# The up projection of a transformer block by seven block products in place of eight

## The chip, the cores and the metric

One core of a Trainium2 chip. The metric is the device time of one execution in microseconds, the median of several runs. One further execution was profiled; its rows carry line numbers of the kernel.

## The reference

One layer of a streaming encoder, on 512 tokens of width 2048, in float32:

```
h = rms_norm(x, pre_mix_g);  z = h @ w_in                       # q, k, v of 8 heads, and the pooled part
m = concat(chunked_attention(z), multiscale_pool(z)) @ w_o
x = x + rms_norm(m, post_mix_g)
h = rms_norm(x, pre_ffn_g)
up = causal_dwconv(h @ w_up, conv_w, conv_b)                    # w_up 2048 x 11264, 3 taps along tokens
y = (gelu(up[..., :5632]) * up[..., 5632:]) @ w_down            # w_down 5632 x 2048
x = x + rms_norm(y, post_ffn_g)
```

## The kernel before

Every matrix product runs on TensorE in the type float32r, each operand split in a high part (rounded by ScalarE, `split`, L127) and a low part (the rest, by VectorE, L128). `mm3` (L143 to L145) multiplies high by high, high by low and low by high, three matmuls into the same bank of PSUM. Each matmul loads 128 x 128 weights and streams up to 512 columns.

Activations lie transposed: 16 tiles of 128 channels by 512 tokens, high and low (`hT`, here called gT). The up projection makes 22 units. A unit is 256 columns of the gate half of w_up and the 256 columns that they are multiplied with; a half unit is one of these two. For a half unit `up` takes four weight tiles of 4 x 128 rows by 256 columns (512 KB each) from a list whose loads run four tiles ahead (`Weights`: SP issues the load into `raw4`, 5 buffers; the split goes to `w4`, 8 buffers, so 4 pairs), and makes 16 x 2 x 3 = 96 matmuls of 512 tokens into two banks. `conv` (L696 to L700) then multiplies by the norm's factor R on VectorE, and adds the three taps on ScalarE and VectorE; `gate` adds the gelu, `product` multiplies the two parts and has POOL store the unit to DRAM (`gd`). Unit 0 is made earlier, beside the norm.

`residual` runs eight times after units 4 to 11: it loads half a token block of x and of the mixing's output, adds them on VectorE and stores them, three blocks to `out` and the last one to `x2d`.

The product with w_down already works by seven products of blocks for eight (Strassen's scheme in Winograd's form), 20 units in five groups: `right` loads blocks of w_down (1 MB, `raw1`, `raw2`), sums them on VectorE and splits them (`wh`, `wl`); `left` does the same with the stored units; `multiply` makes 24 matmuls of 512 columns; `keep_product` has POOL add the products to sums in DRAM by adding DMAs. The first two products (`firsts`) are made right behind the up projection, before the memory of the up stage is given to the pool `p4`. The last two units are multiplied plainly at the end (`last`), block by block, with the last norm; three token blocks reach `out` by adding stores from POOL, the fourth is added to x2 on VectorE.

The order of TensorE's instructions is the order of the program. That of the other engines is chosen by the framework's scheduler when the kernel is built, from priorities in program order and from what is ready; each engine then runs its own list strictly in that order. Buffers are handed out by tag, so that a load waits until the users of an older tile of its tag are done.

Of the kernel before, what the change touches and what calls it, by code (L numbers as in the profile page):

```python
# [15 lines left out]
P = 128  # L16
# [12 lines left out]
WARM = 9  # L29
CU = 4  # L30
# [43 lines left out]
def encoder_layer(ctx: ExitStack, tc: tile.TileContext, x, xT, vecs, rel, post_ffn,  # L74
# [129 lines left out]
    NU = KF // 2  # L204
# [7 lines left out]
    R = const.tile([P, S], F32, name="R")  # L212
# [267 lines left out]
    x2d = dram.tile([P, D], F32, name="x2d")  # L480

    with tc.tile_pool(name="p2", bufs=2, reuse_waits="tile") as p2:
# [102 lines left out]
        for kb in range(KD):  # L585
            if kb % 4 == 0:
                w = [weights.get(f"w{p}0_{kb // 4}") for p in range(2)]
            if kb + 2 < KD:
                x2(kb + 2)
            for p in range(2):  # L590
                for j in range(2):
                    mm3(ups[p][j], part(w[p], kb % 4, slice(j * P, (j + 1) * P)), blk(hT, kb),
                        kb == 0, kb == KD - 1)
# [26 lines left out]
    later = {}  # L620

    def weight(tag, bufs, n, name):

        if n % (bufs + 1) == bufs:
            return later[tag](name, F32R)
        return pr.tile([P, CU, S], F32R, tag=tag, bufs=bufs, name=name)

    def right(c, cc):

        def load(j, l):  # L630
            b = later["raw2"](f"b{j}{l}") if j else raw1(f"b{j}{l}")
            r, cs = 256 * CU * c, slice(l * C + cc * S, l * C + (cc + 1) * S)
            nc.sync.dma_start(b, w_down[r:r + 256 * CU, cs].rearrange(
                "(u j p) n -> p u j n", j=2, p=P)[:, :, j, :])
            return b

        b = {}
        order = yield
        while True:
            i = order  # L640
            for jl in {1: (11, 12), 7: (22,), 6: (22,), 3: (22,), 2: (21,), 4: (21,)}.get(i, ()):
                if jl not in b:
                    b[jl] = load(jl // 10 - 1, jl % 10 - 1)
            if c == cc == 0 and i == 2:
                b[22] = load(1, 1)
            if i == 5:
                nc.vector.tensor_sub(b[11], b[11], b[12])  # L647
            if i == 7:
                nc.vector.tensor_sub(b[12], b[22], b[12])  # L649
            if i == 6:  # L650
# [4 lines left out]
            n = weight.n = getattr(weight, "n", -1) + 1  # L655
            hi, lo = weight("wh", 3, n, "bh"), weight("wl", 2, n, "bl")
            split(hi, lo, v)
            order = yield hi, lo
# [33 lines left out]
    with tc.tile_pool(name="p3", bufs=2, reuse_waits="tile") as p3:  # L692
        def conv(ps, b, tag):
            v = [col(V_CONV, 4 * b + i) for i in range(4)]
            z = p3.tile([P, S], F32, tag="z", name="z")
            nc.vector.tensor_mul(z, ps, R)  # L696
            c = p3.tile([P, S], F32, tag=tag, name=tag)
            nc.scalar.activation(c, z, AF.Identity, scale=v[2], bias=v[3])
            nc.vector.scalar_tensor_tensor(c[:, 1:], z[:, :S - 1], v[1], c[:, 1:], op0=ALU.mult, op1=ALU.add)
            nc.vector.scalar_tensor_tensor(c[:, 2:], z[:, :S - 2], v[0], c[:, 2:], op0=ALU.mult, op1=ALU.add)  # L700
            return c

        def up(u, p, between=None):
            ps = [bank(f"up{u}_{p}_{j}") for j in range(2)]
            for i in range(4):
                w = weights.get(f"w{p}{u}_{i}")
                for kb in range(4 * i, 4 * i + 4):
                    for j in range(2):
                        mm3(ps[j], part(w, kb % 4, slice(j * P, (j + 1) * P)), blk(hT, kb), kb == 0, kb == KD - 1)
                if between and i == 0:  # L710
                    between()
            return ps

        def gate(u, ps):
            a = []
            for j in range(2):
                a.append(conv(ps[j], 2 * u + j, "ca"))
                nc.scalar.activation(a[j], a[j], AF.Gelu_apprx_tanh)
            return a

        def product(u, a, ps):
            g = p3.tile([P, 2, S], F32, tag="g", name="g")
            for j in range(2):
                nc.vector.tensor_mul(g[:, j, :], a[j], conv(ps[j], KF + 2 * u + j, "cb"))
# [5 lines left out]

        def spread2():
            spread(psr, rt)
            nc.vector.tensor_copy(R, psr)

        def residual(t, i):
# [5 lines left out]
            nc.sync.dma_start(x2d[:, cs] if t == NT - 1 else out[t * P:(t + 1) * P, cs], xr)  # L741
# [17 lines left out]

        g1 = up(1, 0, spread2)  # L760
        product(0, gate(0, ups[0]), ups[1])
        product(1, gate(1, g1), up(1, 1))
# [5 lines left out]
        a = gate(NU - 1, up(NU - 1, 0))  # L768
        last = up(NU - 1, 1)

        rights = right(0, 0)
        next(rights)
        firsts = [(i, l, rights.send(i)) for i, l in zip(ORDER0, first_left())]
        product(NU - 1, a, last)
# [3 lines left out]
    with tc.tile_pool(name="p4", bufs=2, reuse_waits="tile") as p4:  # L778
# [8 lines left out]
        later["wh"], later["wl"] = ring("wh", (CU, S), 1), ring("wl", (CU, S), 1)  # L787
# [3 lines left out]
        for r in (slot_h, half_g, later["wl"], later["wh"], raw2, scratch, slot_l, product_part):  # L791
# [81 lines left out]
        spare = [lambda: raw1("wb", F32R)] + [lambda: later["wh"]("wb", F32R), lambda: later["wl"]("wb", F32R)]  # L873
        for k, (cb, i) in enumerate((cb, i) for cb in range(1, 4) for i in range(2)):
            if k < 3:
                w = spare[k]()
            else:
                w = pr.tile([P, CU, S], F32R, tag=("wh", "wl", "wh")[k - 3], bufs=(3, 2, 3)[k - 3], name="wb")
            ws[i, cb] = last_w(i, cb, w)
# [33 lines left out]
        def last(t, cols):  # L913
# [25 lines left out]
            if t < NT - 1:  # L939
# [5 lines left out]
            for cols, vg in sorted(parts[t], key=lambda p: p[0].stop - p[0].start):  # L945
                res = x2_last[cols.start // 1024][:, cols.start % 1024:(cols.stop - 1) % 1024 + 1]
# [12 lines left out]
        x2_last = [row((slot_h, slot_l)[i], f"x2_{i}") for i in range(2)]  # L959
        for i in range(2):  # L960
            nc.sync.dma_start(x2_last[i], x2d[:, i * C:(i + 1) * C])
# [3 lines left out]
        for t in range(2):  # L965
            for cols in blocks(t)[2:]:
                last(t, cols)
            if not t:
                with tc.issue_after(last.mul):
                    for u in range(2):  # L970
                        nc.vector.tensor_add(y[u + 2][:, C:], s16[u], s57[u])
                        nc.vector.tensor_add(y[u + 2][:, :C], s16[u], s74[u])
        for t in range(2, 4):
# [41 lines left out]
```

## Time and profile before

| | us |
|---|---|
| runs | 2020.34, 2020.94, 2021.55 |
| median | 2020.94 |
| profiled execution | 2020.79 |
| its span on the core | 2019.0 |

Instructions are grouped by line, engine and form; after the bar stand the busy time, the mean of one in ns, and the engine's idle time before them with what ended it. PE is TensorE's matmuls and PEld its weight loads, DVE VectorE, ACT ScalarE, POOL GpSimd, SP the queue of plain DMAs. q0 are DMAs that POOL issues, q1 those of SP and ACT. Rows in order of time give start and duration in us. The mean granted TensorE clock of the profiled execution is 0.994.

### The profile page before, as it was taken

What the parts mean: (1) busy time and instruction counts of PE and PEld (TensorE: products, weight loads), DVE (VectorE), ACT (ScalarE), POOL (GpSimd) and SP (SyncE); (2) the same over time, 40 slices, a digit from 0 to 9 for tenths busy, and PEclk for the clock granted to TensorE, in tenths of its full rate; (3) what the DMA queues carried; (4) which work ended last, traced back from release to release, by engine and by line L of the source; (5) the groups of instructions that cost most, each with busy time, mean ns of one, the idle gap of its engine ahead of it and who ended that gap; (6) DMA issues with size and microseconds to landing.
All of it is one profiled execution on the core that took longest, in us unless ns stands there. A gap on an engine that the chain in (4) does not pass through costs nothing.

```text
span 2019.0 us, 22240 instructions
## 1 busy us (share of the span) xinstructions
PE 1992.3 (99%) x8858; PEld 1642.2 (81%) x8858; DVE 1123.6 (56%) x1242; ACT 747.8 (37%) x918; POOL 211.1 (10%) x265
## 2 busy tenths in 40 slices
PE   9999999999999999999999999999999999999997
PEld 7888888888887888888888888888888778888885
DVE  5555255542258644444444444444444898898866
ACT  6333233342244322222222222223222565465443
POOL 4000000001135000000000000000000112222211
PEclk9999999999999999999999999999999999999998
DMA  7332332342355433444444433333332779999997
GB/s 234 115 94 86 94 93 74 94 130 98 101 172 170 132 109 110 151 151 148 144 136 138 144 105 109 116 109 105 105 114 103 224 207 257 237 215 233 213 217 189
DMA packets 228647, 291.59 MB, mean 144 GB/s; under 512 B 9152, under 2 KB 167744, under 8 KB 227264
## 3 DMA queue, kind: packets, MB, share of 16 engines
q1 hardware_dynamic: 204128, 234.59, 36.6%
q0 software_dynamic: 22112, 51.39, 12.8%
q10 hardware_dynamic: 2304, 4.20, 0.6%
q8 instruction: 69, 1.13, 0.2%
q14 instruction: 34, 0.28, 0.0%
HBM read 229.32 MB, written 60.82 MB: 144 GB/s over the span
## 4 chain that ended last, share of the span: by engine, by line
PE 62%; DVE 2%; issue 2%; DMA 2%; ACT 0%; POOL 0%; POOLq 0%; DVEq 0%; SPq 0%; ACTq 0%
PE up L144 16%; PE up L143 15%; PE up L145 15%; PE p L145 5%; PE p L143 5%; PE p L144 5%; DMA wr<-in_w_down 1%; DMA gc<-gd 1%; DVE bl L128 1%; DMA out<-vg 0%; DVE part L678 0%; DVE al L128 0%; DVE b L649 0%; POOL out L943 0%; ACT bh L127 0%
## 5 line engine op out<-in xcount | busy, mean ns | idle before, releaser
L144 PE MATMUL p<-bl,ah 128*128 128x512 f32 x560 | 221.5, 396 | 5.6 <-DVE bl L128 5.6
L143 PE MATMUL p<-bh,ah 128*128 128x512 f32 x560 | 222.4, 397 | 0.8 <-ACT bh L127 0.8
L145 PE MATMUL p<-bh,al 128*128 128x512 f32 x560 | 222.6, 398 | 0.0
L128 DVE TENSOR_TENSOR bl<-b,bh 128x2048 fp32r<-128x2048 f32 x70 | 159.4, 2287 | 21.5 <-PE p L144 11.1
L127 ACT ACTIVATE bh<-b 128x2048 fp32r<-128x2048 f32 x70 | 133.0, 1914 | 64.8 <-DVE b L647 37.7
L128 DVE TENSOR_TENSOR w_2l<-w_2r,w_2h 128x1024 fp32r<-128x1024 f32 x44 | 55.5, 1262 | 161.9 <-ACT w_2h L127 161.8
L144 PE MATMUL up<-gTl,w_1h 128*128 128x512 f32 x352 | 138.1, 392 | 2.7 <-DVE gTl L131 2.7
L144 PE MATMUL up<-gTl,w_0h 128*128 128x512 f32 x352 | 137.4, 390 | 1.1 <-DVE gTl L131 1.0
L143 PE MATMUL up<-gTh,w_1h 128*128 128x512 f32 x352 | 137.5, 391 | 0.0
L145 PE MATMUL up<-gTh,w_1l 128*128 128x512 f32 x352 | 137.5, 391 | 0.0
L143 PE MATMUL up<-gTh,w_0h 128*128 128x512 f32 x352 | 137.2, 390 | 0.1
L145 PE MATMUL up<-gTh,w_0l 128*128 128x512 f32 x352 | 137.0, 389 | 0.0
L145 PE MATMUL up<-gTh,w_3l 128*128 128x512 f32 x352 | 136.9, 389 | 0.0
L143 PE MATMUL up<-gTh,w_2h 128*128 128x512 f32 x352 | 136.9, 389 | 0.0
L144 PE MATMUL up<-gTl,w_2h 128*128 128x512 f32 x352 | 136.9, 389 | 0.0
L145 PE MATMUL up<-gTh,w_2l 128*128 128x512 f32 x352 | 136.9, 389 | 0.0
L143 PE MATMUL up<-gTh,w_3h 128*128 128x512 f32 x352 | 136.9, 389 | 0.0
L144 PE MATMUL up<-gTl,w_3h 128*128 128x512 f32 x352 | 136.9, 389 | 0.0
L144 PEld LDWEIGHTS p<-bl,ah 128*128 128x128 f32 x560 | 105.9, 189 | 32.8 <-DVE bl L128 7.2
L128 DVE TENSOR_TENSOR w_1l<-w_1r,w_1h 128x1024 fp32r<-128x1024 f32 x44 | 53.9, 1224 | 132.6 <-ACT w_1h L127 132.6
L143 PEld LDWEIGHTS p<-bh,ah 128*128 128x128 f32 x560 | 106.0, 189 | 25.6 <-ACT bh L127 1.3
L145 PEld LDWEIGHTS p<-bh,al 128*128 128x128 f32 x560 | 105.9, 189 | 25.5
(377 smaller groups left out, 4181.7 us busy)
## 6 DMA issues: line engine op xcount, KB each, us to landing
b<-in_w_down SPq DMA_DIRECT2D x40, 1024.0 KB, 8.2
sum<-part POOLq DMA_DIRECT2D x70, 512.0 KB, 8.3
w_0r<-in_w_up SPq DMA_DIRECT2D x44, 512.0 KB, 3.5
w_1r<-in_w_up SPq DMA_DIRECT2D x44, 512.0 KB, 4.3
w_2r<-in_w_up SPq DMA_DIRECT2D x44, 512.0 KB, 3.5
w_3r<-in_w_up SPq DMA_DIRECT2D x44, 512.0 KB, 3.5
gd<-g POOLq DMA_DIRECT2D x40, 256.0 KB, 3.2
gc<-gd SPq DMA_DIRECT2D x10, 1024.0 KB, 11.7
```

The source lines that it names most:

```text
L127: rounded = nc.scalar.activation(hi, src, AF.Copy)
L128: nc.vector.tensor_sub(lo, src, f32(hi))
L143: nc.tensor.matmul(ps, l[0], r[0], start=first, stop=False)
L144: nc.tensor.matmul(ps, l[0], r[1], start=False, stop=False)
L145: nc.tensor.matmul(ps, l[1], r[0], start=False, stop=last)
```

## The change

The units 0 to 2 are made as before; units 3 to 21 by blocks. A half unit is a product of w_up's 2048 x 256 (transposed: two column halves m, two channel halves kh) with the 2048 x 512 activations (two channel halves, two token halves). Seven products of 128 columns x 1024 channels x 256 tokens stand in for eight, each with 8 x 3 = 24 matmuls of 256 tokens.

Of the activations' sums, made once on VectorE (`h_sums`), three are kept in the buffers that are later used for w_down's factors (tags raw1, wh, wl), and one difference is written over its block of hT (`h_difference`). The weights' sums are made per half unit by DMAs: SP loads three blocks of w_up (x, y, z; 512 KB, each contiguous in DRAM in the new layout), and POOL issues three adding DMAs that add further blocks onto x and y in SBUF; one sum (product 3) is made on VectorE. `Factors` orders the products so that products 6 and 3 of a half unit come during the next one, loads ten places ahead and splits four ahead. The results are combined out of four banks (`keep_six`, `keep_all`), with signs carried by a second copy of R, -R.

w_up is rearranged outside the program into contiguous blocks. The buffers for w_down's factors are two each beside the up stage and the rest behind it. The third token block's residual, too, is kept in `x2d` and added on VectorE.

```diff
+NU = KF // 2
+PLAIN = 3
-    for u in range(NU):
-        gate, up_ = (halves(f"w{p}{u}", w_up, p * F + u * 256, 4, 256) for p in range(2))
+    for u in range(PLAIN):
+        gate, up_ = ([(f"w{p}{u}_{i}", w_up[u, p, :, i // 2, :, i % 2 * 512:(i % 2 + 1) * 512].rearrange(
+            "m p c -> p m c"), 2, 512) for i in range(4)] for p in range(2))
...
-        return pr.tile([P, CU, S], dt, tag="raw1", bufs=3, name=name)
+    def right_tile(tag, name, dt=F32R):
+        n = turns[tag] = turns.get(tag, -1) + 1
+        if later and n % (2 + LATER[tag]) >= 2:
+            return later[tag](name, dt)
+        return pr.tile([P, CU, S], dt, tag=tag, bufs=2, name=name)
+    LATER = {"raw1": 1, "wh": 2, "wl": 1}
...
+        T = S // 2
+        hs = {i: [pr.tile([P, 8, T], F32R, tag=tag, bufs=2, name=f"h{i}{p}") for p in "hl"]
+              for i, tag in ((4, "raw1"), (7, "wh"), (6, "wl"))}
+        def quarter(k, t, i):
+            return tuple(hT[p][2 * k + i][:, :, t * T:(t + 1) * T] for p in range(2))
...
+        def h_sums(i):
...
+            b11, b12 = whole(0, 0), whole(0, 1)
+            nc.vector.tensor_sub(b11, b11, b12)
+            differences.append(b11)
+            b22 = whole(1, 1)
+            nc.vector.tensor_sub(b12, b22, b12)
+            keep(7, b12)
+            nc.vector.scalar_tensor_tensor(b22, b11, -1.0, b22, op0=ALU.mult, op1=ALU.subtract)
+            keep(6, b22)
+            b21 = whole(1, 0)
+            nc.vector.scalar_tensor_tensor(b21, b22, -1.0, b21, op0=ALU.mult, op1=ALU.subtract)
+            keep(4, b21)
...
+        class Factors:
+            RAW, AHEAD = 10, 4
...
+                    if k in (0, n - 1):
+                        o = [(k, 5), (k, 4), (k, 1), (k, 2), late[0], (k, 7), late[1]]
+                    else:
+                        o = [(k, 4), (k, 1), (k, 2), late[0], (k, 5), (k, 7), late[1]]
...
+                if i == 5 and k in self.alone:
+                    raw("x", raw_x("wx"), 1, 1)
+                    self.add(k, "x", 1, 0)
+                elif i == 4:
+                    raw("w" if k in self.alone else "x", raw_x("wx"), 1, 1)
+                elif i == 1:
+                    raw("y", raw4("wy"), 0, 0)
+                elif i == 2:
+                    raw("z", raw4("wz"), 0, 1)
+            def add(self, k, what, m, kh):
+                nc.gpsimd.dma_start(self.raw[k, what], self.block(k, m, kh), accum_op=ALU.add)
+            def make(self, k, i):
...
+                if i == 3:
+                    nc.vector.tensor_add(v, v, self.raw[k, "z"])
+                hi, lo = w4("wfh"), w4("wfl")
+                split(hi, lo, v)
+                if i == 4 and k not in self.alone:
+                    self.add(k, "x", 1, 0)
+                elif i == 1:
+                    self.add(k, "y", 1, 0)
+                elif i == 5:
+                    self.add(k, "x", 0, 0)
...
+        def keep_six(k):
+            z = flat(new_z())
+            q6, q57, q12 = (banks.pop((k, n)) for n in ("6", "57", "12"))
+            v2 = z[:, 3 * T:]
+            for v in (v2, z[:, :T]):
+                nc.scalar.activation(v, q12[:, :T], AF.Copy)
+            nc.vector.tensor_add(v2, q6[:, :T], v2)
+            nc.vector.tensor_add(z[:, T:3 * T]..., q57..., v2[:, None, :].to_broadcast([P, 2, T]))
+            nc.vector.tensor_add(v2, q57[:, :T], z[:, 2 * T:3 * T])
+            nc.vector.tensor_add(z[:, :T], q12[:, T:], z[:, :T])
+        def keep_all(k):
+            nc.vector.tensor_add(z[:, T:3 * T], banks.pop((k, "34")), z[:, T:3 * T])
+            nc.vector.tensor_mul(z, z, flat(RR))
...
+        def seven(k, i):
+            w = factors.get()
+            ps, half = half_bank(k, i)
+            for kb in range(8):
+                mm3(ps[:, half], part(w, kb), h_factor(i, kb), kb == 0, kb == 7)
...
-        for u in range(2, NU - 1):
-            a = gate(u, up(u, 0))
-            product(u, a, up(u, 1))
-            if 4 <= u < 12:
-                residual(*divmod(u - 4, 2))
...
+        for k, i in factors.order:
+            seven(k, i)
+            if (k, i) == (end - 1, 3):
+                next_first()
+            if i == 6:
+                keep_six(k)
+                if k == end:
+                    next_first()
+            if i == 3:
+                keep_all(k)
+                if 4 <= k < 20 and k % 2:
+                    residual(*divmod(k // 2 - 2, 2))
         firsts = [(i, multiply(l, r)) for i, l, r in firsts]
...
-        for r in (slot_h, half_g, later["wl"], later["wh"], raw2, scratch, slot_l, product_part):
+        for r in (scratch, product_part, raw2, later["wl"], later["raw1"], half_g, slot_h, slot_l, later["wh"]):
...
-            if t < NT - 1:
+            if t < 2:
...
+    up_blocks = w_up[0].reshape(2, 8, P, 2, NU, 2, P).transpose(4, 3, 5, 0, 2, 1, 6).reshape(NU, 2, 2, 2, P, 8 * P)
```

More of the change, by code (lines that the diff above doesn't have):

```diff
@@ L700, in conv, with new_z, flat, gate @@
             nc.vector.scalar_tensor_tensor(c[:, 2:], z[:, :S - 2], v[0], c[:, 2:], op0=ALU.mult, op1=ALU.add)
[L701 to L715, printed above, removed]
+        def new_z():
+            return p3.tile([P, 2, S], F32, tag="z", name="z")
+        def flat(v):
+            return v.rearrange("p a b -> p (a b)")
+        def gate(u, z):
+            a = p3.tile([P, 2, S], F32, tag="ca", name="ca")
             for j in range(2):
-                a.append(conv(ps[j], 2 * u + j, "ca"))
-                nc.scalar.activation(a[j], a[j], AF.Gelu_apprx_tanh)
-            return a
-        def product(u, a, ps):
-            g = p3.tile([P, 2, S], F32, tag="g", name="g")
+                taps(z[:, j, :], 2 * u + j, a[:, j, :])
+            nc.scalar.activation(flat(a), flat(a), AF.Gelu_apprx_tanh)
+            return a
+        def product(u, g, z):
             for j in range(2):
-                nc.vector.tensor_mul(g[:, j, :], a[j], conv(ps[j], KF + 2 * u + j, "cb"))
+                c = p3.tile([P, S], F32, tag="cb", name="cb")
+                taps(z[:, j, :], KF + 2 * u + j, c)
+                nc.vector.tensor_mul(g[:, j, :], g[:, j, :], c)
             if u < NC * CU:
```

157 lines of the change are left out of this document (121 added, 36 removed).

## The prediction

> **What bounds the kernel now.** I read the summary of the profile first, then the stages (busy time by windows), then the order of time on TensorE, then the groups by line, the DMA queues, and last the order of time where the up projection hands over to w_down.
>
> ```profile
> span 2019.0 us, 22240 instructions
> PE 1992.3 (99%) x8858; PEld 1642.2 (81%) x8858; DVE 1123.6 (56%) x1242; ACT 747.8 (37%) x918; POOL 211.1 (10%) x265
> ```
> ```profile
> core 0: us, PE busy (x) PEld busy (x) DVE busy (x) ACT busy (x) POOL busy (x), PEclk, DMA share, GB/s
> 1000.00:1100.00 100.00, 100.00 (x443) 82.81 (x442) 42.92 (x48) 27.07 (x30) 2.95 (x5) 1.00 0.46 144
> 1700.00:1800.00 100.00, 100.00 (x433) 80.79 (x432) 91.14 (x61) 53.89 (x49) 21.47 (x18) 1.00 0.98 230
> 1557.60:1600.00 42.40, 38.93 (x159) 30.51 (x158) 41.61 (x32) 23.44 (x23) 5.21 (x6) 0.96 0.74 230
> ```
>
> The first two windows are the up projection and w_down (which already uses seven products). In both TensorE is full; in the up projection VectorE is at 43% and the DMA engines at 46%, in w_down they are at 91% and 98%, and TensorE still loses nothing. So the end is set by the number of matmuls times their pace, and by the few stalls where the stages meet (third window: 159 matmuls in 42.4 us).
>
> The busy time of a matmul is not its pace, since they overlap. The pace is read from starts:
>
> ```profile
> 999.63 0.39 PE L143 MATMUL up<-gTh,w_1h 128*128 128x512 f32 x1
> ...
> 1011.87 0.39 PE L143 MATMUL up<-gTh,w_3h 128*128 128x512 f32 x1
> ...
> 2001.07 0.28 PE L143 MATMUL yl<-wb,gh 128*128 128x256 f32 x1
> ...
> 2003.83 0.27 PE L145 MATMUL yl<-wb,gl 128*128 128x256 f32 x1
> ```
> ```profile
> 584.67 3.25 PE L533 MATMUL mt<-ident,mg 128*128 128x128 f32 x28
> ```
>
> Between the first two rows lie 54 steps in 12.24 us: 226.7 ns for 512 columns. Between the last two lie 23 steps in 2.76 us: 120.0 ns for 256 columns. Half the columns cost 53% of the pace.
>
> **The change part by part.** *Matmuls.* A half unit (gate or value part of one unit) is 96 matmuls of 512 columns (16 blocks x 2 column blocks x 3 of the split). It becomes 7 products x 8 blocks x 3 = 168 of 256 columns. 19 units are 38 half units: 3648 x 226.7 ns = 826.9 us go, 6384 x 120.0 ns = 766.1 us come: **-60.8 us**. (The order of the built program has 2736 more TensorE rows, just this difference.) In arithmetic one eighth is saved, 103 us; 42 of them are eaten by the 13.3 ns that each matmul costs beyond its columns at either width (226.7 - 2 x 106.7, 120.0 - 106.7, with 106.7 the difference of the two paces).
>
> The Trainium skill, "TensorE: Matmul & The Clock Gate", Back-to-back issue gap, gives N/2.4 + 2.5 ns, that is 215.8 and 109.2 ns; by it the change would save 90 us. The rows above disagree with it by some 11 ns at either width and decide.
>
> A half unit now lasts 20.16 us, one product 2.88. All that follows has to fit in that.
>
> *VectorE and ScalarE.*
>
> ```profile
> L128 DVE TENSOR_TENSOR w_2l<-w_2r,w_2h 128x1024 fp32r<-128x1024 f32 x39 | 47.8, 1226 | 152.9 <-ACT w_2h L127 152.9
> L814 DVE TENSOR_TENSOR gc<-gc,gc 128x1024 f32<-128x1024 f32 x5 | 6.1, 1222 | 0.1
> L696 DVE TENSOR_TENSOR z<-up,R 128x512 f32<-128x512 f32 x78 | 53.5, 692 | 102.3 <-PE up L145 102.3
> L922 DVE TENSOR_TENSOR y<-yl,y 128x256 f32<-128x256 f32 x2 | 0.8, 416 | 0.0
> L699 DVE SCALAR_TENSOR_TENSOR ca<-z,vec,ca 128x511 f32<-128x511 f32 x40 | 28.1, 745 | 0.0
> L724 DVE TENSOR_TENSOR g<-ca,cb 128x512 f32<-128x512 f32 x38 | 24.5, 685 | 0.0
> L740 DVE SCALAR_TENSOR_TENSOR xr<-mr,rm,xr 128x1024 f32<-128x1024 f32 x8 | 10.3, 1284 | 30.3 <-DMA mr<-mtokd 30.3
> L127 ACT ACTIVATE w_2h<-w_2r 128x1024 fp32r<-128x1024 f32 x39 | 41.4, 1062 | 170.8 <-PE up L144 170.8
> L698 ACT ACTIVATE ca<-z,vec 128x512 f32<-128x512 f32 x40 | 30.2, 802 | 0.0
> L718 ACT ACTIVATE ca<-ca 128x512 f32<-128x512 f32 x38 | 24.1, 634 | 37.0 <-DVE ca L700 36.5
> L924 ACT ACTIVATE junk<-y 128x256 f32<-128x256 f32 x2 | 0.8, 409 | 0.8 <-DVE y L922 0.8
> ```
>
> Per unit (40.3 us) VectorE has 14 splits x 1.226, 2 sums for product 3 x 1.222, per half unit 3 adds of 256 (0.416) and 2 of 512 (0.692) out of the banks and one multiplication of 1024 by R (1.222), then 8 taps x 0.745 and 2 gating products x 0.685: 17.2 + 2.4 + 5.3 + 2.4 + 6.0 + 1.4 = 34.7 us, 86% (before 19.9 in 43.5). With a residual (1.28) 36.0, 89%. ScalarE: 14 x 1.062 + 4 x 0.802 + 4 x 0.409 and a gelu of twice 0.634 at most: 21 us, 52%. I follow VectorE's new order through a half unit: in the three products after product 3 of the half unit before (8.6 us) it has 9.8 to 11 us of work, so it falls 1 to 2.5 us behind, and in the four products after that (11.5 us) it has 9 to 10 us and catches up. Factors are made three to four products (8.6 to 11.5 us) ahead, so the lag reaches no matmul: cost 0. If that cover went, each us that VectorE is late in a half unit costs 38 us.
>
> *DMA.*
>
> ```profile
> q0 software_dynamic: 9800, 18.89, 56.0%
> q1 hardware_dynamic: 11424, 26.22, 41.2%
> sum<-part POOLq DMA_DIRECT2D x35, 512.0 KB, 8.3
> ```
>
> This is the window 1700 to 1900, where q0 carries only adding DMAs: 56% of 200 us for 18.89 MB (36 of 0.524 MB) is 3.11 us of all 16 engines for one; a plain load, 41.2% for 26.22 MB, is 1.65. A half unit has 3 loads, 3 adds and half a g store of 0.524 MB (at the load's price 0.8): 4.95 + 9.33 + 0.8 = 15.1 us of 20.16, 75%; where a residual runs, 2.5 more, 87%. Above it is 98% with TensorE fed. But those adds go from SBUF to DRAM; adds from DRAM into SBUF do not occur in this trace. Bounds: a plain load's 1.65 below, and no end above that a row gives; I take 3.11, the one row of an add. The add onto raw tile x is issued when split 4 is done, some 7 us before product 4 itself starts, and holds nothing if it lands within 13 us, and no matmul within 15 us; the row has 8.3 us to landing under a busier DMA. The split waits in ScalarE's queue, behind which stand the taps and the bank copies, and VectorE's low half waits on it. POOL's queue holds the adds in the order wanted; the g store in front of the last add waits for a product that is done by then. The SP queue waits, where a residual borrows two of the five raw buffers, until product 3 two half units back is made: that leaves the load of y about 6 us before its split. Cost of all this 0; if an add took over 15 us, its excess per half unit.
>
> *Entry.* Sums of the activations: 16 operations and 6 splits, 22 x 1.22 = 27 us of VectorE, in three plain half units of 21.8 us with half of VectorE free, and the difference blocks written once the first half of the last plain half unit has read them. I count 65 VectorE operations, 74 us, in the 87 us of the four. 0 to 5, taken as 2 us.
>
> *Handover to w_down.* This is where the change gives back.
>
> ```profile
> 1557.91 0.40 PE L143 MATMUL p<-bh,ah 128*128 128x512 f32 x1
> 1570.12 0.50 PE L143 MATMUL p<-bh,ah 128*128 128x512 f32 x1 [0.83 <-ACT bh L127]
> 1572.91 0.51 PE L144 MATMUL p<-bl,ah 128*128 128x512 f32 x1 [2.30 <-DVE bl L128]
> ...
> 1575.35 0.63 PE L144 MATMUL p<-bl,ah 128*128 128x512 f32 x1
> 1575.78 0.63 PE L145 MATMUL p<-bh,al 128*128 128x512 f32 x1
> ```
> ```profile
> 1565.94 1.23 DVE L814 TENSOR_TENSOR gc<-gc,gc 128x1024 f32<-128x1024 f32 x1
> 1567.08 1.22 DVE L811 SCALAR_TENSOR_TENSOR s<-s,gc 128x1024 f32<-128x1024 f32 x1
> ...
> 1570.57 2.29 DVE L128 TENSOR_TENSOR bl<-b,bh 128x2048 fp32r<-128x2048 f32 x1
> 1578.32 6.69 DVE L128 TENSOR_TENSOR bl<-b,bh 128x2048 fp32r<-128x2048 f32 x3
> ```
>
> Before, two products of w_down were ready when the up projection ended (1557.91), and the third waited 3.1 us for VectorE; by 1600 some 159 matmuls had started, which at w_down's pace (433 in 100 us, 231 ns) is 36.7 of 42.1 us: 5.4 lost, the slower pace at 1575 (0.43 us) included. Now the buffers that hold w_down's first factors are full of activation sums (h4, h7, h6) until the last products 4, 7 and 6. Say T is the end of the last up product. In the new VectorE order, at starts 1.14 (1024) and 2.2 us (2048) apart as in the rows above, the low half of the first factor (bl in the rows) is done at T - 0.5, so product one starts on time. Before the second stand the multiplication by R, an add of 2048, four taps, an add: T + 8.7, stall 3.1. Before the third stand the rest of both halves of the last unit (taps, gating: to T + 15.8), six operations of w_down's left side, the split: T + 24.9, while TensorE is through at T + 14: stall 10.9. Before the fourth 7.7 us of VectorE against 5.4: stall 2.5. Together 16.5, and 1.5 for the slower pace after it, against 5.4: **+12.6**, taken as 12 (0 if the planner's order is not what holds TensorE, 20 if the loads behind it are late too).
>
> *The end.* The residual of the third token block is added by VectorE (4 x 0.745) instead of ScalarE and an adding store; VectorE has that time between blocks of 2.7 us with 1.4 of work each. 0 (-2 to +2). *Layout of w_up*: loads of 2 and 4 KB runs for 1 KB; the DMA is not late in this stage, 0.
>
> Sum against the profiled execution (2020.79 us, span 2019.0; the median of the runs is 2020.94): 2020.8 - 60.8 + 2 + 12 = **1974 us**.
>
> **The rivals.** *Slower: the adds bound the stage.* If an add into SBUF costs P of all engines, a half unit needs 5.8 + 3P; from P = 4.8 TensorE waits, and from P = 5.2 (38 x 1.2 = 47 us) the gain is gone. At twice the row, 6.2, a half unit is 24.4 us: 38 x 4.2 = +161, 2135 us. For it: no row has this direction, and three adds hang in a chain of splits. Against: 67% more than the price of the nearest row is needed, which held at 98% of the DMA. 0.13.
>
> *The pace of 120 ns does not hold for 168 in a row.* The longest run of 256 columns is 24 matmuls, after 512-wide ones, so that TensorE's queue may have been full ahead of it. 28 pairs of load and matmul in a row took 3.25 us, at most 116 ns each, after a wait, which speaks against a slower issue; the pace of 512 does move, between 226 and 231 ns (443 and 433 matmuls in 100 us). With 4 ns more: +26, 2000; with 7: +45, 2019. 0.09. The Trainium skill, same page, "Wait — 56ns, not 53.3ns?", has some 62 ns of sequencer time for a matmul when the hardware decoder is off; if a weight load costs the same, 124 ns, which is the +26; no row here shows that time by itself.
>
> *VectorE is the bound.* At 15% more than the sum (waits between ScalarE and VectorE that I did not see): 41.4 for 40.3 us, 19 units: +20, 1994. For it: 89%; against: it ran at 91% in w_down with TensorE full. 0.07.
>
> That the program does other than it says is excluded by the order.
>
> **How the numbers follow.** My forecast has 0.71, with 1962 to 1988 of its own from the bounds of handover and entry. The range is 1960 to 2004: it takes in the rivals' milder halves, and leaves out under 2 in 10. This measurement tells 0.2% (4 us) from no change: faster 0.83 (forecast, VectorE, milder pace), same 0.02, slower 0.15 (adds, the worst of the pace).
>
> **What would show it.** Right: 168 matmuls per 20.2 us between 740 and 1510 us at 256 columns, starts 120 ns apart; VectorE 80 to 90% and DMA 70 to 90% there; the stage's end near 1500; then a wait of some 10 us for a low half of w_down's third factor. Wrong: waits of TensorE for low halves of the factors inside the stage, ScalarE's splits waiting on the adds with landings above 15 us, or starts over 124 ns apart.

## Result and the profile after

| | before | after |
|---|---|---|
| runs, us | 2019.84 to 2021.55 (4) | 1959.49 to 1962.54 (4) |
| median, us | 2020.64 | 1960.87 |
| profiled execution (span), us | 2020.79 (2019.0) | 1959.49 (1957.6) |

The ratio is 0.970, 95% interval 0.969 to 0.972. The change saves 61.3 us between the profiled executions, where 46.8 were forecast. The median lies inside the range given (1960 to 2004), 0.9 us above its lower end.

The summary of the profile after, and three of its stages (columns as before: busy time and count of PE, PEld, DVE, ACT, POOL, then granted clock, DMA share, GB/s):

```profile
span 1957.6 us, 28601 instructions
PE 1928.9 (99%) x11594; PEld 1722.0 (88%) x11594; DVE 1407.3 (72%) x1575; ACT 890.5 (45%) x1092; POOL 311.5 (16%) x377
...
760.00:1490.00 730.00, 730.00 (x6091) 730.00 (x6091) 594.46 (x694) 357.53 (x416) 120.74 (x143) 1.00 0.76 189
1496.70:1535.00 38.30, 26.76 (x95) 20.21 (x94) 37.21 (x33) 20.95 (x20) 2.01 (x3) 0.82 0.41 152
1600.00:1700.00 100.00, 100.00 (x433) 80.98 (x432) 87.78 (x57) 54.41 (x50) 20.89 (x18) 1.00 0.97 229
```

The first window is the up projection by seven products: TensorE without a gap, VectorE busy 594 of 730 us (81%), the DMA engines 76%. The second is the handover: VectorE is busy 37.2 of 38.3 us, TensorE 26.8. The third is w_down, as before.

Where the stages meet, in the order of time on TensorE after, with one row of before:

```profile
731.42 0.28 PE L145 MATMUL q<-gTh,wfh 128*128 128x256 f32 x1
...
1496.74 0.39 PE L145 MATMUL p<-bh,ah 128*128 128x512 f32 x1
...
1902.85 0.39 PE L145 MATMUL yl<-wb,gh 128*128 128x512 f32 x1
...
1947.42 0.28 PE L147 MATMUL yl<-wb,gl 128*128 128x256 f32 x1
```
```profile
1959.15 0.40 PE L143 MATMUL yl<-wb,gh 128*128 128x512 f32 x1
```

The time between the first and second row is 765.3 us for 6384 matmuls: 119.9 ns each. This gives the account, stage by stage:

| stretch | before | after | change | forecast |
|---|---|---|---|---|
| to the first matmul of the fourth unit (before: 3648 matmuls ahead of 1557.91) | 731.0 | 731.4 | +0.4 | +2 |
| 38 half units | 826.9 | 765.3 | -61.6 | -60.8 |
| first matmul of w_down to first of the last block | 401.2 | 406.1 | +4.9 | +12 |
| last block, to its last matmul | 44.7 | 44.6 | -0.1 | 0 |
| last matmul to end of span | 15.2 | 10.2 | -5.0 | 0 |
| sum | 2019.0 | 1957.6 | -61.4 | -46.8 |

Two terms were mis-sized, both to the same side: the handover by 7 us and the end by 5. The stretch from the first matmul of w_down to the last block holds the handover and the rest of w_down.

**The handover.** After, on TensorE (the bracket is the wait before and what ended it):

```profile
1506.05 0.50 PE L146 MATMUL p<-bl,ah 128*128 128x512 f32 x1 [2.99 <-DVE bl L130]
...
1508.28 0.63 PE L147 MATMUL p<-bh,al 128*128 128x512 f32 x1
1508.71 0.63 PE L145 MATMUL p<-bh,ah 128*128 128x512 f32 x1
...
1512.83 0.39 PE L147 MATMUL p<-bh,al 128*128 128x512 f32 x1
1519.77 0.79 PE L145 MATMUL p<-bh,ah 128*128 128x512 f32 x1 [6.55 <-ACT bh L129]
1522.57 0.80 PE L146 MATMUL p<-bl,ah 128*128 128x512 f32 x1 [2.00 <-DVE bl L130]
```

The waits are those of the forecast: the second product 3.0 us, the third 8.6 (6.6 for ScalarE's high half, 2.0 for VectorE's low half), none before the first. Behind each wait some matmuls start 0.43 us apart (1508.28 to 1508.71) where 0.23 is usual. Summed over all starts in w_down that lie over 0.30 us apart, less 0.2325 each, 16.8 us are lost; the forecast had 18.0. What the forecast had too small is what the kernel before lost in the same stage:

```profile
1609.79 0.50 PE L144 MATMUL p<-bl,ah 128*128 128x512 f32 x1 [0.99 <-DVE bl L128]
...
1617.59 0.77 PE L144 MATMUL p<-bl,ah 128*128 128x512 f32 x1 [1.96 <-DVE bl L128]
...
1619.01 0.63 PE L144 MATMUL p<-bl,ah 128*128 128x512 f32 x1
```

By the same sum 10.8 us were lost there, not 5.4: 5.8 by 1600, where the window that the forecast had read ended, and 5.0 at the ninth and tenth product behind it. In the profile after no product behind the third waits. So the stalls grew by 6.0 us. The stage grew by 4.9 only, since its other starts take 389.3 us in sum for 390.4; this 1.1 us is there in every profile with units by seven products against every one without, and its cause stays open.

How much is lost at the ninth and tenth product differs from one execution to the next. The other two runs whose up projection is all plain (layout_only and tail_only, below) lost 2.1 and 3.6 us there, 8.5 and 9.4 in all; the variants of the change below lose between nothing and 4.4.

**The end.** The last operations of VectorE and the stores behind them, before and after, and the DMA engines in that stretch:

```profile
2008.72 0.42 DVE L922 TENSOR_TENSOR y<-yl,y 128x256 f32<-128x256 f32 x1
...
out<-vg POOLq DMA_DIRECT2D x2, 512.0 KB, 7.7
out<-x SPq DMA_DIRECT2D x3, 256.0 KB, 4.4
...
2003.80:2019.00 15.20, 0.30 (x3) 0.10 (x1) 8.26 (x18) 4.93 (x12) 2.51 (x4) 0.60 0.83 180
```
```profile
1949.80 0.41 DVE L1123 TENSOR_TENSOR y<-yl,y 128x256 f32<-128x256 f32 x1
...
out<-x SPq DMA_DIRECT2D x3, 256.0 KB, 2.1
...
1947.40:1957.60 10.20, 0.31 (x3) 0.10 (x1) 5.99 (x14) 1.74 (x6) 0.54 (x1) 0.67 0.32 118
```

Before, VectorE takes the last block 4.9 us after the last matmul (2003.83), and the last stores need 4.4 us to land, beside two adding stores of 512 KB still under way, with the DMA engines at 83%. After, these are 2.4 us, 2.1 us and 32%.

### The profile page after: what moved, and what is told of

Same layout as the page of the kernel before. It is cut to its first block, busy times and chain, and to the rows that moved or that the text cites. A ratio compares the mean times of both kernels' runs of the same rounds, so it can differ in the third digit from the quotient of the medians.

```text
span 1957.6 us, 28601 instructions
## 1 busy us (share of the span) xinstructions
PE 1928.9 (99%) x11594; PEld 1722.0 (88%) x11594; DVE 1407.3 (72%) x1575; ACT 890.5 (45%) x1092; POOL 311.5 (16%) x377
## 4 chain that ended last, share of the span: by engine, by line
PE 64%; DVE 2%; DMA 1%; issue 1%; ACT 0%; POOL 0%; POOLq 0%; DVEq 0%; ACTq 0%
PE q L146 13%; PE q L147 13%; PE q L145 13%; PE p L145 7%; PE p L147 7%; PE p L146 7%; PE up L146 2%; PE up L147 2%; PE up L145 2%; DMA out<-vg 0%; DMA a<-gd 0%; DVE bl L130 0%; DVE x L1148 0%; PE yl L145 0%; DVE wfl L130 0%
## 5 line engine op out<-in xcount | busy, mean ns | idle before, releaser
L146 PE MATMUL q<-gTl,wfh 128*128 128x256 f32 x1216 | 344.0, 283 | 0.0
L147 PE MATMUL q<-gTh,wfl 128*128 128x256 f32 x1216 | 343.9, 283 | 0.0
L145 PE MATMUL q<-gTh,wfh 128*128 128x256 f32 x1216 | 343.8, 283 | 0.0
L147 PEld LDWEIGHTS q<-gTh,wfl 128*128 128x128 f32 x1216 | 233.1, 192 | 0.0
L145 PEld LDWEIGHTS q<-gTh,wfh 128*128 128x128 f32 x1216 | 233.1, 192 | 0.0
L146 PEld LDWEIGHTS q<-gTl,wfh 128*128 128x128 f32 x1216 | 232.9, 192 | 0.0
L129 ACT ACTIVATE wfh<-wx 128x1024 fp32r<-128x1024 f32 x152 | 158.8, 1056 | 120.3 <-PE q L146 82.1
L130 DVE TENSOR_TENSOR wfl<-wx,wfh 128x1024 fp32r<-128x1024 f32 x152 | 183.9, 1220 | 35.5 <-ACT wfh L129 35.5
L130 DVE TENSOR_TENSOR wfl<-wy,wfh 128x1024 fp32r<-128x1024 f32 x76 | 92.7, 1220 | 26.3 <-ACT wfh L129 25.9
L146 PE MATMUL q<-h4l,wfh 128*128 128x256 f32 x304 | 86.0, 283 | 0.0
```

Of the source, the lines that this page charges most:

```text
L129: rounded = nc.scalar.activation(hi, src, AF.Copy)
L130: nc.vector.tensor_sub(lo, src, f32(hi))
L145: nc.tensor.matmul(ps, l[0], r[0], start=first, stop=False)
L146: nc.tensor.matmul(ps, l[0], r[1], start=False, stop=False)
L147: nc.tensor.matmul(ps, l[1], r[0], start=False, stop=last)
```

## The experiments

Three questions are asked: whether the pieces of the account belong to the edits that they are put down to; how much of VectorE and of the DMA engines the stage had left, which the forecast took as enough; and what bounds the handover. Ratios are to the kernel before, run on the same chip at the same time, with the 95% interval. Differences to the change are between medians from different chips, on which the medians of the kernel before lie between 2020.6 and 2022.5 us; differences of 2 us and less are read from the traces alone.

### The end: with the old one, and the new one alone

```diff
 tail_old (on after)
-            if t < 2:
+            if t < NT - 1:      # and x2d, x2_last for the last block alone
 tail_only (on before): the reverse
```

> The changed kernel with the old end: the third token block's residual goes by adding stores into the output again, scaled on ScalarE, and only the fourth block's is added by VectorE. All else as changed. Theory A (the 5.0 us between the last matmul and the end that the changed kernel has less than the one before, 10.2 for 15.2, come from this edit alone: fewer adding stores in flight under the last stores, and a VectorE that is less late): 1966 us, 5 more than the changed kernel, with 15 us from the last matmul's start to the end and the last store's landing near 4.4 us again. Theory B (the end got shorter for what the seven products changed upstream, such as earlier loads of the sums): 1961, no difference, 10 us at the end.

> The kernel before with the new end alone: the residual of the third token block is kept beside the fourth's and added by VectorE, stored by plain stores; the up projection stays plain. Theory A (the end's 5 us belong to this edit alone, as the changed kernel with the old end, 4.6 us slower, says): 2016, 4 to 5 less than the kernel before, about 10.5 us from the last matmul to the end for 15.2. Theory B (the new end only pays behind the seven products): 2021.

Measured: tail_old 1965.5 us (0.972, 0.970 to 0.974), 4.6 more than the change. tail_only 2016.0 (0.998, 0.997 to 0.999), 4.9 less than before by the medians, 4 by the ratio, with 2 to 6 in its interval. So an end of some 4 to 5 us belongs to this edit, with or without the seven products. The profiled executions show less of it: the last stretch took 13.0 us in tail_old (10.2 in the change) and 13.8 in tail_only (15.2 before). Of its two parts the landing of the last stores follows the edit in each profile: 4.4 us before, 4.5 in layout_only and 3.5 in tail_old with the old end, 2.1 in the change and 2.5 in tail_only with the new one. VectorE's delay behind the last matmul does not: 4.9 us before and 3.5 in tail_old, but 2.4 in the change and 5.2 in tail_only. What sets it was not tried.

### The layout of w_up alone

```diff
 layout_only (on before)
-        gate, up_ = (halves(f"w{p}{u}", w_up, p * F + u * 256, 4, 256) for p in range(2))
+        gate, up_ = ([(f"w{p}{u}_{i}", w_up[u, p, :, i // 2, :, i % 2 * 512:(i % 2 + 1) * 512]... , 2, 512)
```

> The kernel before with w_up laid out in blocks on the host and read in the new layout (loads in runs of 2 KB for 1 KB; the stationary blocks of a weight tile stand in another order), all units plain, the old end. Theory A (the DMA is not late in this stage, so the layout costs and brings nothing): 2021, no difference of 1 us. Theory B (the addresses of the stationary blocks or the longer runs change the pace of the plain units): the 4008 matmuls after the first unit at another pace than 226.7 ns, each ns 4 us.

Measured: 2020.1 us (0.9994, 0.9985 to 1.0004): no difference. The pace of the plain matmuls is 226.7 ns in both.

### Fewer units by seven products

```diff
 ten_units
-PLAIN = 3
+PLAIN = 12
...
```

The sums of the activations move to the last plain half units, and the residuals start two half units earlier in the count of those by seven products.

> The changed kernel with the last 10 units by seven products for 19 (the first 12 plain), the sums of the activations in the last three plain half units as before. Theory A (each half unit saves the same 1.6 us: 96 x 226.7 ns = 21.76 go and 168 x 119.9 = 20.14 come; entry, handover and end cost the same once): 18 half units fewer, 29.2 us more than the changed kernel, 1990. Theory B (the saving is bought with something fixed, say a faster entry or end that has nothing to do with the count): the time per half unit would be below 1.6, and ten units would lose less than 29: at half of it 1975.

Measured: 1995.6 us (0.987, 0.986 to 0.989), 34.7 more than the change. In the profile 35.4 more: the first matmul of w_down starts at 1527.2 for 1496.7, of which 0.6 is there at the fourth unit already and 0.7 is one wait at 1524, so 29.2 for 18 half units, 1.62 each, as A says. But most of the rest, 4.5 us, lies in w_down: 1.4 at the tenth product, and 3.1 in the first four, since TensorE waits for the first product already.

```profile
1530.57 0.50 PE L146 MATMUL p<-bl,ah 128*128 128x512 f32 x1 [3.00 <-DVE bl L130]
```

VectorE is through with that low half 3.3 us after the first matmul of w_down, in the change 0.2; with 10 units the last residual (1.28 us of VectorE and its loads) stands two half units before the end instead of eighteen. That this is the reason was not tried by itself; but the handover is no fixed cost, it depends on how far behind VectorE is when it comes.

### How much of VectorE is left

```diff
 dve_2, dve_4 (N = 2, 4)
-            nc.vector.tensor_mul(z, z, flat(RR))
+            for _ in range(1 + N if k < end - 5 else 1):
+                nc.vector.tensor_mul(z, z, flat(RR))
 vector_sums
-                nc.gpsimd.dma_start(self.raw[k, what], self.block(k, m, kh), accum_op=ALU.add)
+                nc.gpsimd.dma_start(self.raw[k, what], self.block(k, m, kh))
+                if i in (5, 3, 7):          # in make, ahead of the split
+                    nc.vector.tensor_add(v, v, v)
```

> The changed kernel with two more multiplications by R (128x1024, some 1.15 us each from start to start) on VectorE in each half unit but the last five or so (33 of 38); the values become wrong by powers of R. VectorE is busy 594 us of the 730 between 760 and 1490, 16.4 per half unit of 20.15; with 2.3 more it is 18.7, 93%. Theory A (the factors stand three to four products ahead, so VectorE costs nothing until its work itself exceeds a half unit): no change, 1961. Theory B (VectorE's waits on ScalarE, DMAs and banks make it late before that, above all in the eight half units with a residual): waits for low halves inside the stage, each us per half unit 33 us.

> The same with four more multiplications: 16.4 + 4.6 = 21.0 us of VectorE per half unit of 20.15. Theory A (VectorE bounds from where its work exceeds the half unit): 0.8 us in each of 33 half units, +27 us, 1988, with waits for low halves of the factors inside the stage. Theory B (it is late before that): the whole 4.6 less 2 of cover, +85 us, 2046. If neither, and the time stays at 1961, VectorE's cover is larger than its busy time says.

> The changed kernel as it would be with the three sums of weights of a half unit on VectorE: each adding DMA becomes a plain load on the same queue (1.5 us of all DMA engines for 2.9), and VectorE adds 128x1024 in place ahead of the split (1.15 us each). The factors are wrong (the doubled block instead of a sum), the work is that of such a kernel. The two kernels with more VectorE work lost 5.7 us in the stage at 18.7 us of VectorE per half unit (in the half units with a residual alone) and 76.5 at 21.0; here it is 16.4 + 3.45 = 19.85. Theory A (VectorE bounds from about 18.7 of 20.15 us, because it waits in turn for ScalarE, DMAs and banks): between these two, some 45 us in the stage and some 3 at the handover, 2009, with the DMA engines near half of their time. Theory B (VectorE can be filled to 20.15, and the position of the extra work in the two kernels before made them late): 1965 to 1970.

Measured: dve_2 1967.3 us (0.974, 0.972 to 0.975), dve_4 2037.4 (1.008, 1.007 to 1.010), vector_sums 2010.4 (0.995, 0.994 to 0.996). For each, in this order, TensorE's waits from 735 to 1490 (us in all, how many, the longest) and the window 760 to 1490:

```profile
PE q L147 <- DVE wfl L130: 4.4, 5, 1.6
760.00:1490.00 730.00, 725.58 (x6044) 724.59 (x6043) 656.78 (x754) 352.02 (x414) 120.28 (x143) 1.00 0.77 186
```
```profile
PE q L147 <- DVE wfl L130: 50.3, 27, 4.3
760.00:1490.00 730.00, 679.61 (x5470) 673.21 (x5469) 663.20 (x748) 312.17 (x372) 109.46 (x130) 0.97 0.72 169
```
```profile
PE q L147 <- DVE wfl L130: 26.0, 32, 2.8
760.00:1490.00 730.00, 702.39 (x5723) 693.86 (x5722) 659.62 (x753) 327.82 (x389) 80.42 (x137) 0.99 0.54 176
```

The operations of dve_2 add less than was expected: 60 more in the window, 62 us busy, 2.1 us per half unit for 2.3. With them VectorE is at 90% of the window (16.4 + 2.1 = 18.5 us, 92% of a half unit that has them), and the five waits fall between 983 and 1190, about where the residuals are added (884 to 1173). With twice as much it is no busier than 91% (663 of 730), though it now sets the pace: the other 9% are its own waits, 60 of 67 us for ScalarE's high halves. So it is full at some 90 to 92%, and the true margin was about 2 us of 20.15, not 3.7. B was nearer for dve_4 (85 forecast, 76.5 found), A for dve_2. Late half units cost more than the wait: in dve_4 waits of 51 us in the whole stage lengthen it by 76.2, mostly because some 190 matmuls behind the waits started 0.21 us apart instead of 0.12 (18 of the 25 us).

vector_sums, with 90% too, lost 46.9 us in the stage, as A said: with the sums of weights on VectorE the change would be worth 10 us, not 60. The adding DMAs are what makes it pay.

### How much of the DMA engines is left

```diff
 adds_twice
-                nc.gpsimd.dma_start(self.raw[k, what], self.block(k, m, kh), accum_op=ALU.add)
+                for _ in range(2):
+                    nc.gpsimd.dma_start(self.raw[k, what], self.block(k, m, kh), accum_op=ALU.add)
```

> The changed kernel with each adding DMA of w_up issued twice (the factors become A + 2B, so the values are wrong): 6 adds per half unit for 3. In the changed kernel's trace 109 adds took 348.5 us of all 16 engines less 27 to 30 for the stores of g, 2.9 us each, and a plain load 1.5. A half unit then needs 3 x 1.5 + 6 x 2.9 + 0.75 = 22.7 us of 20.15. Theory A (the adds' price on the DMA engines bounds once it passes what is left): +2.5 us in each of 38 half units, +97 us, 2058, with the DMA engines at 95% or more and ScalarE's splits waiting on adds. Theory B (what counts is the chain from a split over the add to the next split, with over 11 us of cover): the landing doubles from 6.7 to over 13 us and each half unit is late by more than the DMA engines' own sum, 2100 or more with the DMA engines at 85% or less. If the time stays at 1961, adds cost the engines less than their packets' time.

Measured: 2189.2 us (1.083, 1.081 to 1.086). The queues of the change between 750 and 1490 (q0 the adding DMAs and the stores of g, q1 the plain loads; MB and share of the 16 engines) with the time to landing of an add, then, of this kernel, TensorE's waits, the window and the same queue from 760 to 1490:

```profile
q0 software_dynamic: 18560, 66.59, 47.1%
q1 hardware_dynamic: 21355, 72.35, 28.1%
...
wx<-in_w_up POOLq DMA_DIRECT2D x73, 512.0 KB, 6.7
```
```profile
PE q L145 <- ACT wfh L129: 84.3, 29, 6.3
PE q L147 <- DVE wfl L130: 18.9, 32, 0.8
760.00:1490.00 730.00, 628.20 (x4704) 614.29 (x4704) 462.17 (x540) 269.51 (x322) 166.06 (x196) 0.90 0.92 208
...
q0 software_dynamic: 26272, 94.93, 70.1%
```

In the change the plain loads take 28.1% of 740 us for 72.35 MB, which is 1.51 us for one of 0.524 MB. The adds take 47.1% of 740 us less 27 us (9.4 MB of g at that price), which is 2.95 us for each of 109. Here it is 70.1% of 730 us, less 20, for 168: 2.93 us. So the price is near that of the nearest row (3.11), and does not grow. w_down began at 1718.6, so a half unit took 26.0 us, for the 23 that the DMA engines need by that sum; they are at 92%, TensorE waits for ScalarE's splits, which wait 402 us for the added tiles between 735 and 1490, and its clock is 0.90 in the window. So neither theory alone: the DMA engines are nearly as full as A says (95%), and the time is past 2100 as B says. That B's chain adds to A's sum is the reading that fits; it was not tried by itself. The forecast's rival with twice the row (2135) would have been too mild, but the point at which adds decide is far from the row measured.

### What bounds the handover

```diff
 in_turn: each factor of w_down's first column block queued behind the last split of the one before
+                        with ExitStack() as queue:
+                            for v in behind:
+                                queue.enter_context(tc.issue_after(v))
                             r = rs.send(i)
 no_taps
+            if b % KF >= KF - 2:
+                return
             nc.vector.scalar_tensor_tensor(c[:, 1:], ...
 sums_on_pool
-                nc.vector.tensor_sub(b[12], b[22], b[12])       # and the sum b[11] + b[22]
+                (nc.gpsimd if c == cc == 0 else nc.vector).tensor_sub(b[12], b[22], b[12])
 add_in_turn: in_turn, and
-                nc.vector.tensor_add(b[11], b[11], b[22])       # first column block
+                    nc.gpsimd.dma_start(b[11], w_down[...], accum_op=ALU.add)
```

> The changed kernel with w_down's third to seventh products of the first column block prepared strictly one after the other on VectorE and ScalarE, so that the low half of the third factor stands ahead of the five operations for later products that are ahead of it now (5.9 us of VectorE). Same operations. Theory A (the handover is bound by the amount of VectorE work between the end of the up projection and some 50 us later, in which VectorE has no pause to speak of): the stall before the third product falls by some 6 us, but later products stall by nearly as much; the time stays within 2 us of 1961. Theory B (it is the third factor's place in VectorE's order alone): 1955, 6 us less. Theory C (w_down's loads are late): no stall moves, 1961.

> The changed kernel without the two earlier taps of the convolution in the last unit (both its gate and its value half): eight VectorE operations of 0.66 us each, 5.3 us, are left out of the work that lies around the handover; nothing else changes. Theory A (handover bound by the amount of VectorE work) and B (by what stands ahead of the third factor) both say 5 us less, 1956, with the stall before the third product at some 4 us for 9.3. Theory C (late loads, or ScalarE): 1961 and no stall moves.

Measured: in_turn 1960.5 us (0.970, 0.968 to 0.972), the same as the change; no_taps 1956.8 (0.968, 0.966 to 0.970), 4.1 less. In no_taps the third product waits 5.3 us instead of 8.6 and the second 1.8 instead of 3.0. In in_turn the third waits 3.4, and later ones wait that did not:

```profile
1517.78 0.79 PE L146 MATMUL p<-bl,ah 128*128 128x512 f32 x1 [3.35 <-DVE bl L130]
...
1533.59 0.51 PE L147 MATMUL p<-bh,al 128*128 128x512 f32 x1 [0.64 <-DVE al L130]
...
1546.00 0.50 PE L146 MATMUL p<-bl,ah 128*128 128x512 f32 x1 [1.07 <-DVE bl L130]
```

Over w_down in_turn gains 1.4 us (404.7 for 406.1), less than the 2.4 by which that stage differs between the profiles of before and layout_only. Taking away 5.3 us of VectorE's work gains 3.8 there (402.3). That is A: the amount of work decides, and its order little.

> The changed kernel with two sums of w_down's blocks (128x2048, for the fourth and fifth product of the first column block) on GpSimd instead of VectorE: 4.4 us of VectorE go from the 35 us after the end of the up projection, in which VectorE has no pause; GpSimd has nothing to do there and needs some 6 us for each (1.5 us per 512 elements in the rows of this kernel), done before the splits that read them are due. Theory A (the amount of VectorE work): up to 4.4 us less, 1957, from the stalls at the fourth and later products and, since VectorE's order moves, partly at the third. Theory B (GpSimd's work slows VectorE's by as much as it takes over, or its stores of the sums come late): 1961. Theory C (only what stands ahead of the third factor counts): 1961, since these sums stand behind it.

> The changed kernel with the factors in turn as in the earlier run, and the sum for w_down's fifth product of the first column block (128x2048) as an adding DMA from w_down instead of an operation of 2.2 us on VectorE; the DMA engines have nothing to do between 1506 and 1520. Theory A (the handover is bound by the amount of VectorE work, and an adding DMA, other than GpSimd's own operation, does not hold VectorE up): 2.2 us less than with the turn alone, 1958, with no operation of VectorE there longer than its kind and the stalls of the fifth and seventh product gone. Theory B (another bound stands right behind, such as w_down's loads or the products before the sums): 1960.5, and the stalls move to a later product.

Measured: sums_on_pool 1971.2 us (0.975, 0.974 to 0.977), 10 more than the change: neither theory. POOL's two sums, the VectorE operation beside them, and TensorE:

```profile
1524.00 4.60 POOL L655 TENSOR_TENSOR b<-b,b 128x2048 f32<-128x2048 f32 x1
1528.56 4.59 POOL L657 TENSOR_TENSOR b<-b,b 128x2048 f32<-128x2048 f32 x1
```
```profile
1523.92 10.31 DVE L130 TENSOR_TENSOR al<-s,ah 128x1024 fp32r<-128x1024 f32 x1
```
```profile
1541.03 0.79 PE L146 MATMUL p<-bl,ah 128*128 128x512 f32 x1 [8.99 <-DVE bl L130]
```

An operation that takes 1.22 us elsewhere took 10.31: VectorE stood still while GpSimd did both of its sums, and these began late, behind two stores in POOL's queue that waited for ScalarE. The fourth product then waited 9 us. The Trainium skill, "SBUF — State Buffer", Who interferes with whom, says that VectorE and GpSimd share a pair of ports under an exclusive lock; the trace agrees, 9.1 us of delay for 9.2 us of GpSimd.

add_in_turn 1960.6 us (0.969, 0.968 to 0.971): no gain over in_turn in the medians or over w_down (405.0 us for 404.7), as B says. The adding DMA held up nothing on VectorE, but the wait moved to the ninth product, behind a load of the stored units:

```profile
1550.24 1.06 ACT L129 ACTIVATE ah<-gc 128x1024 fp32r<-128x1024 f32 x1 [3.74 <-DMA gc<-gd]
```
```profile
1555.49 0.50 PE L146 MATMUL p<-bl,ah 128*128 128x512 f32 x1 [1.82 <-DVE bl L130]
```

So two bounds stand one behind the other: VectorE's work up to some 35 us after the up projection, and from 50 us on the load that lands at 1550. The same load fits the second group of waits of before. Its issue, ScalarE's row that it releases, and the first matmul of the ninth product, in before and after:

```profile
1590.70 0.34 SPq L799 DMA_DIRECT2D gc<-gd  x1
...
1604.55 1.06 ACT L127 ACTIVATE ah<-gc 128x1024 fp32r<-128x1024 f32 x1 [6.10 <-DMA gc<-gd]
...
1608.40 0.40 PE L143 MATMUL p<-bh,ah 128*128 128x512 f32 x1
```
```profile
1540.35 0.34 SPq L1005 DMA_DIRECT2D gc<-gd  x1
...
1550.58 1.06 ACT L129 ACTIVATE ah<-gc 128x1024 fp32r<-128x1024 f32 x1 [2.49 <-DMA gc<-gd]
...
1558.10 0.39 PE L145 MATMUL p<-bh,ah 128*128 128x512 f32 x1
```

The load is there 46.6 us after the first matmul of w_down before (1557.91) and 53.8 after (1496.74), 7.2 later; but the ninth product is due 50.5 us after that matmul before and 61.4 after, 10.9 later, for the longer waits ahead of it. So the load is late before and in time after. The load seems to hang on VectorE's work too: it is issued within 0.1 us of the end of a low half that reads an older tile of the same name (`al<-gc`, done at 1590.7 before, 1540.3 after and 1538.7 in add_in_turn), and then takes 13.8 us to land before, 10.2 after. All this is read from the traces; no run moved the load alone. Of the versions that leave nothing out none beats the change by more than its runs differ.

## Why the prediction was right, and where it was off

- *Matmuls* (-60.8): right, -61.6 found. 119.9 ns held over 6384 in a row, and the rival of another pace is out. It scales by the half unit (ten_units).
- *VectorE* (cost 0): right in the result, TensorE does not wait once between 731.42 and 1496.74. Its share was put at 86% and is 81%, since operations start 1.14 us apart where their rows last 1.22. But the cover was not what lay between 86 and 100%: VectorE is full at some 90 to 92%. And a us of delay in every half unit would cost not 38 us but about half as much again (51 us of waits cost 76 in dve_4), for the slow starts behind each wait. The rival that VectorE is the bound was also worked out wrongly: 41.4 us is 15% more than the 36.0 of a unit with a residual, and only eight of the 19 units have one; for the others it is 39.9 of 40.3, no cost.
- *DMA* (cost 0): right. 75% was worked out (87% beside a residual), 76% found over the stage; 3.11 us for an add, 2.95 found; 8.3 us to landing, 6.7 found.
- *Layout* (0): right, shown alone.
- *Entry* (+2): 0.4.
- *Handover* (+12): the mechanism and the sizes of the waits were right (3.1, 10.9 and 2.5 forecast for the second, third and fourth product, 3.0, 8.6 and none found; the slow starts behind each wait, put at 1.5 us, took up part of the next one). The step that failed is "against 5.4": what the kernel before lost at the same place was read from a window that ended too early. It lost 10.8 in that execution, and the second half of that went away; the stalls of the change lost 16.8 for the 18.0 forecast. So the handover cost 6.0 us more than before, not 12.6, and w_down with it 4.9.
- *The end* (0, -2 to +2): the step that failed asked only whether VectorE has time for the operations that are added. What the edit takes away was not priced: two scalings of 1024 on ScalarE and two adding stores of 512 KB that were under way beneath the last stores. It is worth some 4 to 5 us alone. That the stores beneath are what slows the last ones is read from the landing times.

The forecast's own range (1962 to 1988) was missed by 1 us, since both mis-sized terms erred to the same side. The wider range held by 0.9 us; every rival that it was widened for is slower, and no reason is given for the 2 us that it adds below, so that it held there is luck. The bounds of the handover (0 to 20) held, those of the end (-2 to +2) did not.

## What to carry to other kernels

When a stage is bound by the count and pace of matmuls, price the change by the pace read from starts, and then look at the engine that takes over the saved work: it is full before its busy time says 100%. A stall that a change adds is to be set against all stalls that it replaces, to the point where both traces run alike again, not to the first quiet window, and in more than one execution. An edit at the end of a kernel is priced by what it removes from beneath the last stores as well as by what it adds.

## What the runs showed of the hardware

- GpSimd's additions of two operands in SBUF stopped a VectorE operation of that kind: 1.22 us became 10.31 (sums_on_pool). An adding DMA issued by the same engine did not (add_in_turn).
- After most waits of 2 us and more, 6 to 13 matmuls of 512 columns start 0.43 us apart for 0.23 (256 columns: 0.21 for 0.12). Not after all: none did behind the 3.0 us at 1530.57 in ten_units. The granted clock of the window 1496.7 to 1535 in the change is 0.82.
- An adding DMA from DRAM into SBUF takes 2.95 us of all DMA engines for 512 KB, twice a plain load (1.51), and a little less than one from SBUF into DRAM (3.11).
